# Score tiles in three shared PSUM banks and a second bank for filling work, in the grouped-query attentions of a two-layer trunk

## The chip, the cores and the metric

One core of one Trainium2 chip runs the whole program in one launch. The metric is the device time of one execution in microseconds (us); lower is better. TensorE does the matrix products, VectorE (DVE), ScalarE (ACT) and GpSimd (POOL) the elementwise work, SyncE (SP) issues most of the DMAs.

## The reference, cut to what matters

Two layers of a parallel-branch trunk over 512 latent tokens and 256 context tokens, width 1024. Each layer normalises and modulates the tokens, projects them once, runs a neighbourhood attention (A) and a grouped-query attention (B, 8 heads of 64 channels, keys of 256 context and 512 latent tokens), multiplies each branch by its own SiLU gate path, projects and merges. The second layer updates the latent tokens alone. What the change touches is branch B:

```
def _attend(q, k, v):
    s = jnp.einsum('bqkgd,btkd->bkgqt', q, k).astype(jnp.float32) * (HEAD_DIM ** -0.5)
    p = jax.nn.softmax(s, axis=-1).astype(v.dtype)
    return jnp.einsum('bkgqt,btkd->bqkgd', p, v)
...
qb = _rope_2d(_rmsnorm(hs(b_q, GQA_Q_HEADS), q_norm_b), pos_row, pos_col)
b_att = _gqa_latent(qb, k_all, v_all)     # latent queries: 768 keys
...
o_a = (a_att * jax.nn.silu(a_z)) @ w_o_a
o_b = (b_att * jax.nn.silu(b_z)) @ w_o_b
merged = jax.nn.sigmoid(g_a) * o_a + jax.nn.sigmoid(g_b) * o_b
return merged @ w_out
```

In the first layer the 256 context queries also attend, to the 256 context keys.

## The kernel before

All products of float32 data are made of two or three products of high and low parts (`mm3`: L435, L436, L437), so TensorE has most of the work.

The grouped-query attention of a layer goes head by head, heads 0 to 7. For a head, `gq_scores` makes four **score tiles** of 128 queries by 768 keys, here called i0 to i3. A tile is four matmuls (L886 and L887, high and low keys; 512 and then 256 columns, since one matmul writes at most one PSUM bank of 512 float32). VectorE then reads the tile for its row maximum (L1157), ScalarE reads it again for the exponential (L1158, with the row sum read out behind it), ScalarE casts the result to fp16 (`h`, L837), and VectorE (i0 and i2) or GpSimd (i1 and i3, `SPLIT_POOL`) makes the fp16 **low part** (L838). SyncE turns the pair by a transposing DMA (`ht<-h`, L842). When all four tiles of the head are turned, `gq_values` spreads the reciprocal row sums by four small transposes (`divide`, L849) and makes the head's **values** by twelve matmuls (L1174 and L1175), which ScalarE and VectorE then gather (`head_out`, L824 and L825). The first layer has a fifth, smaller score tile for each head: `ctx_scores`, 256 context queries by 256 keys in a 512-column tile, with its maximum (L899, L901), two exponentials (L905) and `ctx_values` (L921).

Between the heads stands **filling work** (`fill`): the rest of the gate projections (`g_chunks`, out of `hx` tiles) and branch A's output projection (`o_chunks("a", ...)`, out of `gah` and `gal`), in pieces (`chan_proj`) of 24 or 12 matmuls that each accumulate in one PSUM bank and are then emptied by ScalarE's tanh (L625) or VectorE's multiply (L703). `pipeline` writes the order of the program: scores of head h, values of head h-1, an eighth of the filling pieces; before the last head's values it writes what is left of them.

The written order isn't the order that runs. A scheduler in the build simulates the program and sets the order on each engine by it; what is ready earliest goes first. It also sets the semaphores: an instruction waits for the last reader of a PSUM region that it overwrites, and regions of one tile that lie in the same bank are not told apart.

PSUM has eight banks for each partition. Throughout, `f` (1 bank, filling) and `t` (2 banks, transposes and values) stay open; `open_ps` opens the other five for each stage. In the grouped-query attentions these are two score tiles of 1024 columns, of which 768 are used (`s`, 4 banks), and `v` (1 bank). `psw` hands out the banks of projections in turn from `f` and the `x` banks; there are no `x` banks here, so all filling pieces take `f`, but for one that `v_for` sends to `v`.

Of the kernel before, what the change touches and what calls it, by code (L numbers as in the profile page):

```python
# [72 lines left out]
def hybrid_kernel(es: ExitStack, tc, x, ctx, cvec, w_ada, w_ada0, small, gvec, w_in, w_o_a, w_o_b, w_out,  # L73
# [13 lines left out]
    def nm(s):  # L87
        uid[0] += 1
        return f"{s}_{uid[0]}"
# [4 lines left out]
    pm = {}  # L94

    def ps_pool(stack, kind, bufs, cols):
        pool = tc.tile_pool(name=nm("ps" + kind), bufs=bufs, space=bass.MemoryType.PSUM, reuse_waits="tile")
        pm[kind] = (stack.enter_context(pool), cols)
# [6 lines left out]
    def open_ps(x=0, **kinds):  # L105

        if "es" in pm:
            pm["es"].close()
        pm["es"] = ExitStack()
        pm["n"], pm["i"], pm["v_for"] = x + 1, 0, ()  # L110
        if x:
            kinds["x"] = (x, 512)
        for kind, (bufs, cols) in kinds.items():
            ps_pool(pm["es"], kind, bufs, cols)

    def psw(n=512, kind="w"):
        if kind == "w":
            kind = "f" if pm["i"] % pm["n"] == 0 else "x"
            pm["i"] += 1
            if pm["i"] in pm["v_for"]:  # L120
                kind = "v"
        pool, cols = pm[kind]
        return pool.tile([128, cols], F32, tag=kind, name=nm("ps" + kind))[:, :n]
# [154 lines left out]
    def ada_steps(l, tiles, halves, nv, pool, queue=None):  # L278

        cb = {}  # L280

        def load(h):
            cb[h] = pool.tile([128, 2, 512], F32, tag="cb", name=nm("cb"), bufs=1)
            for v in range(nv):
                src = cd[8 * v + 4 * h:8 * v + 4 * h + 4].rearrange("k p -> (k p)").unsqueeze(0)
                nc.sync.dma_start(cb[h][:, v, :], src.to_broadcast([128, 512]))

        def load_tile(h, i):
            cb["w"] = pool.tile([128, 512], F32, tag="rawb", name=nm("rawb"), bufs=2)
            (queue or nc.sync).dma_start(cb["w"], w_ada[l, h, i])  # L290

        def dot(h, i, v):
            if v == 0:
                load_tile(h, i)
            w = cb["w"]
            o = w if v == nv - 1 else pool.tile([128, 512], BF16, tag="junk", name=nm("junk"), bufs=1)
            behind(ON_DVE, lambda: V.tensor_tensor_reduce(o, w, cb[h][:, v, :], 1.0, 0.0, ALU.mult, ALU.add,
                                                          asum[:, i, h, v:v + 1]))
        res = []
        for h in halves:  # L300
            res += [lambda h=h: load(h)] + [lambda h=h, i=i, v=v: dot(h, i, v) for i in tiles for v in range(nv)]
        return res
# [6 lines left out]
    def ada_mod(l):  # L309
        mod_finish(l, ada_sum(0, 16, 2).rearrange("p (a k) v -> p a k v", a=2), 0, 8)  # L310
# [179 lines left out]
    def run(fill, n):  # L490
        for _ in range(min(n, len(fill))):
            fill.pop(0)()
# [102 lines left out]
    def layer(l, hx, nxt, start):  # L595
        first = l == 0
# [7 lines left out]
        def gate_steps(halves, pool):  # L604
            return (ada_steps(l, range(16, 24), halves, nv, pool)
                    + ([lambda: ada_gate(l, nv, pool)] if 1 in halves else []))
# [9 lines left out]
        att = {}  # L616
# [90 lines left out]
        if first:  # L707
            w, pss = start()
# [21 lines left out]
            bg = ada_steps(1, range(16), (0,), 2, hp["p"])  # L730
        else:
# [5 lines left out]
            bg = gate_steps((0, 1), hp["p"])  # L737
# [49 lines left out]
        if True:  # L787
            def softmax_tail(p, n, r, total, pieces, on_act=False):

                V.reciprocal(r, r)  # L790
                V.tensor_scalar(r, r, P_UP, None, ALU.mult)
                for i, (c0, c1) in enumerate(pieces):
                    if on_act:
                        S.activation(p[:, c0:c1], p[:, c0:c1], AF.Copy, scale=r[:, i:i + 1])
                    else:
                        V.tensor_scalar(p[:, c0:c1], p[:, c0:c1], r[:, i:i + 1], 0.0, ALU.mult, ALU.add,
                                        accum_out=total[:, 1:2])
# [85 lines left out]
            def scores(ps, q, kh, kl, cuts):  # L883

                for c0, n, sl in cuts:
                    T.matmul(ps[:, c0:c0 + n], q, sl(kh), start=True, stop=False)  # L886
                    T.matmul(ps[:, c0:c0 + n], q, sl(kl), start=False, stop=True)  # L887

            def cut(a, b):
                return lambda k: k[:, a:b]  # L890

            def ctx_scores(q, kh, kl, ct, late=True):

                pss = ps_score()
                for i in range(2):
                    scores(pss, q[:, 512 + 128 * i:640 + 128 * i], kh, kl,
                           [(256 * i, 256, cut(512, 768))])
                mx = sp.tile([128, 2], F32, tag="mx", name=nm("mx"), bufs=8)
                V.tensor_reduce(mx, pss.rearrange("p (i n) -> p i n", i=2), AX, ALU.max, negate=True)  # L899
                if late:  # L900
                    V.tensor_scalar(mx, mx, P_LOG, None, ALU.add)  # L901
                p = p_tile()
                r = sp.tile([128, 2], F32, tag="r", name=nm("r"), bufs=8)
                for i in range(2):
                    S.activation(p[:, 256 * i:256 * i + 256], pss[:, 256 * i:256 * i + 256], AF.Exp,  # L905
                                 bias=mx[:, i:i + 1], accum_out=r[:, i:i + 1])
                if not late:
                    softmax_tail(p, 512, r, mx, [(0, 256), (256, 512)])
                turned(p, 512, ct.rearrange("p a i k n -> p (a i k) n"), G)
                return ct, r  # L910
# [14 lines left out]
            def p_tile():  # L925
                return att["p"].tile([128, att["w"]], F32, tag="p", name=nm("p"), bufs=att["np"])

            def ps_score(n=512):
                return psw(n, "s")
# [83 lines left out]
            def pipeline(fill, spread, scores_of, values_of, last=None, bg=[]):  # L1013

                n = len(fill)
                prev = None
                for h in range(8):
                    att["bg"] = bg if h > 3 or pm["n"] == 1 else []
                    st = scores_of(h)
                    if prev is not None:  # L1020
                        values_of(h - 1, prev)
                    run(fill, len(fill) - (n - n * min(h + 1, spread) // spread))
                    prev = st
                if last is not None:
                    run(fill, len(fill))
                    last()
                run(bg, len(bg))
                att["spare"] = True
                values_of(7, prev)
                run(fill, len(fill))  # L1030
# [24 lines left out]
            bg = []  # L1055
# [43 lines left out]
            bg = gate_steps((0,), hp["p"]) if first else []  # L1099
# [38 lines left out]
                turn_late(1 if i == 0 else 0)  # L1138
            bp_es.close()
            gq_es = open_att(f"gq{l}", 768, NP_GQ[l], 0, NH_GQ[l])  # L1140
            open_ps(s=(2, 1024), v=(1, 512))
            if first:
                pm["v_for"] = (2,)
            nc.sync.dma_start(zb.rearrange("p (f n) -> p f n", f=4)[:, :, :ntok], zs[:, :, :ntok])
            V.memset(vbig[:, 2950:2951], -P_LOG)
            lift = vbig[:, 2950:2951].to_broadcast([128, 768])
# [1 line left out]
            def gq_scores(q, kh, kl):  # L1148
                ht = att["p"].tile([128, 4, 12, 128], F16, tag="ht", name=nm("ht"), bufs=2)
                r = att["p"].tile([128, 4], F32, tag="r4", name=nm("r4"), bufs=3)  # L1150
                for i in range(4):
                    pss = ps_score(768)
                    scores(pss, q[:, 128 * i:128 * i + 128], kh, kl,
                           [(0, 512, cut(0, 512)), (512, 256, cut(512, 768))])
                    p = p_tile()
                    mx = sp.tile([128, 2], F32, tag="mx", name=nm("mx"), bufs=8)
                    V.tensor_tensor_reduce(p, pss, lift, -1.0, 3e38, ALU.add, ALU.min, mx[:, 0:1])  # L1157
                    S.activation(p, pss, AF.Exp, bias=mx[:, 0:1], accum_out=r[:, i:i + 1])  # L1158
                    turned(p, 768, ht[:, i], G if i in SPLIT_POOL else V)
                    run(att["bg"], 1)  # L1160
                return ht, r
# [38 lines left out]
            bg = gate_steps((1,), Parts(att["p"], own)) if first else []  # L1200
# [3 lines left out]
        with tc.tile_pool(name=f"mrg{l}", bufs=1, reuse_waits="tile") as mp:  # L1204
# [34 lines left out]
            bg = ada_steps(1, range(16), (1,), 2, mp, G) + [lambda: ada_mod(1)] if first else []  # L1239
            run(bg, 1)  # L1240
            per_bg = -(-len(bg) // nt)
            for n in range(2):
# [14 lines left out]
                late = []  # L1257
# [187 lines left out]
    def nxt():  # L1445
        if not hx1:
            hx1.extend([[big("hx") for _ in range(2)] for _ in range(2)])
        return hx1
    layer(0, hx0, nxt, start)
    layer(1, hx1, None, None)  # L1450


# [73 lines left out]
```

## Time and profile before

| | us |
|---|---|
| median of 3 runs (lowest, highest) | 1110.4 (1109.44, 1111.03) |
| the profiled execution | 1110.55 |
| its span in the trace | 1108.8 |
| TensorE busy | 1074.5 (97%) |
| VectorE, ScalarE, GpSimd busy | 767.4, 617.2, 470.1 |
| first grouped-query attention, in the trace | about 374 to 545 |
| second grouped-query attention | about 920 to 1040 |

The page gives busy time by engine. A view by windows gives it for a stretch, with the clock that the throttle granted to TensorE (1.00 is full). The view of waits adds up how long an engine stood idle before a group of instructions and what ended that. In rows of the timeline the first number is the start and the second the duration, in us; matmuls overlap their neighbours, so the distance between two starts, not the duration, is what one costs.

### The profile page before, as it was taken

Reading aid. Unit: us, or ns where it says so; the run is one execution under the profiler, and the core shown is the slowest. Engines: PE = TensorE matmul, PEld = TensorE weight load, DVE = VectorE, ACT = ScalarE, POOL = GpSimd, SP = SyncE. Lnnn points to the kernel's source line nnn. Section 1 sums busy time; section 2 is a strip of 40 time slices with the busy share of each in tenths; the row PEclk is TensorE's granted clock in tenths of the full one; section 3 lists DMA queues with packets and bytes.
Section 4 is the critical chain, followed back from the end, with each engine's and each line's share of the span. In section 5 each row is a group of like instructions: output and inputs, shape, how many; then the busy total and the mean of one; then the engine's idle time right before and its main releaser. Section 6 shows DMA issues by size and latency. Waiting matters only on the chain. (4 is left out here: it accounts for less than half of the span.)

```text
span 1108.8 us, 16943 instructions
## 1 busy us (share of the span) xinstructions
PE 1074.5 (97%) x5672; PEld 876.9 (79%) x5672; DVE 767.4 (69%) x1600; ACT 617.2 (56%) x1236; POOL 470.1 (42%) x397
## 2 busy tenths in 40 slices
PE   8999999899999999979999999999999999999998
PEld 6688888788888877757788878888877888777677
DVE  5567799974378478676577785466997665777473
ACT  6464279776333566655330275444899446786430
POOL 1044235554256244454521455232355472564531
PEclk9999999999999999989999999999999999999999
DMA  9454325554543498769533542453565536879642
GB/s 374 153 169 143 91 70 116 125 137 121 174 141 117 132 205 185 172 185 271 171 105 125 166 136 82 138 165 99 132 148 130 156 106 171 200 232 236 188 152 77
DMA packets 236001, 171.79 MB, mean 155 GB/s; under 512 B 160141, under 2 KB 201865, under 8 KB 234249
## 3 DMA queue, kind: packets, MB, share of 16 engines
q1 hardware_dynamic: 228576, 156.31, 51.7%
q0 software_dynamic: 2368, 7.87, 2.2%
q10 hardware_dynamic: 4968, 6.53, 1.8%
q8 instruction: 45, 0.74, 0.3%
q14 instruction: 44, 0.35, 0.1%
HBM read 115.58 MB, written 17.32 MB: 120 GB/s over the span
## 5 line engine op out<-in xcount | busy, mean ns | idle before, releaser
L838 POOL TENSOR_TENSOR h<-p,h 128x256 f16<-128x256 f32 (+2 forms) x104 | 113.1, 1096 | 167.7 <-ACT h L837 119.9
L422 POOL TENSOR_TENSOR wlo<-raw,whi 128x512 fp32r<-128x512 f32 x70 | 98.8, 1416 | 124.5 <-ACT whi L420 80.9
L435 PE MATMUL psf<-hx,whi 128*128 128x512 f32 (+1 forms) x360 | 137.5, 382 | 2.5 <-ACT zt L625 1.3
L437 PE MATMUL psf<-hx,wlo 128*128 128x512 f32 (+1 forms) x360 | 135.5, 376 | 0.0
L436 PE MATMUL psf<-hx,whi 128*128 128x512 f32 (+1 forms) x360 | 135.4, 376 | 0.0
L435 PE MATMUL psx<-whi,hx 128*128 128x512 f32 (+1 forms) x328 | 121.0, 372 | 0.0
L420 ACT CAST whi<-raw 128x512 fp32r<-128x512 f32 x136 | 82.9, 620 | 67.5 <-DMA raw<-in_w_in_dram 48.3
L437 PE MATMUL psx<-whi,hx 128*128 128x512 f32 (+1 forms) x328 | 120.0, 367 | 0.0
L436 PE MATMUL psx<-wlo,hx 128*128 128x512 f32 (+1 forms) x328 | 119.6, 366 | 0.0
L408 POOL TENSOR_TENSOR wlo<-raw,whi 128x512 fp32r<-128x512 f32 x40 | 59.5, 1489 | 119.2 <-ACT whi L405 76.0
L405 ACT CAST whi<-raw 128x512 fp32r<-128x512 f32 x88 | 54.2, 623 | 96.8 <-PE psx L437 34.2
L508 POOL TENSOR_TENSOR ss<-ss,ehalf 128x8 f32<-128x8 f32 (+2 forms) x40 | 63.6, 1593 | 77.8 <-DVE ss L505 72.5
L422 DVE TENSOR_TENSOR wlo<-raw,whi 128x512 fp32r<-128x512 f32 x66 | 70.8, 1073 | 35.2 <-ACT whi L420 34.1
L837 ACT CAST h<-p 128x256 f16<-128x256 f32 (+2 forms) x136 | 81.6, 616 | 7.7 <-DMA ct<-h 3.7
L435 PEld LDWEIGHTS psf<-hx,whi 128*128 128x128 f32 x360 | 67.8, 188 | 15.1 <-ACT zt L625 2.5
L1157 DVE CUSTOM_DVE_ANT_0 p<-pss,vb 128x768 f32<-128x768 f32 x64 | 60.4, 954 | 25.4 <-PE pss L887 22.7
L1158 ACT ACTIVATE p<-pss,mx 128x768 f32<-128x768 f32 x64 | 57.6, 901 | 35.7 <-DVE mx L1157 34.8
L437 PEld LDWEIGHTS psf<-hx,wlo 128*128 128x128 f32 x360 | 67.8, 188 | 11.8
L436 PEld LDWEIGHTS psf<-hx,whi 128*128 128x128 f32 x360 | 67.9, 189 | 10.7
L437 PEld LDWEIGHTS psx<-whi,hx 128*128 128x128 f32 x328 | 61.9, 189 | 10.2
L436 PEld LDWEIGHTS psx<-wlo,hx 128*128 128x128 f32 x328 | 62.0, 189 | 9.4
L435 PEld LDWEIGHTS psx<-whi,hx 128*128 128x128 f32 x328 | 61.8, 189 | 9.1 <-issue 0.2
(338 smaller groups left out, 2972.4 us busy)
## 6 DMA issues: line engine op xcount, KB each, us to landing
raw<-in_w_in_dram SPq DMA_DIRECT2D x168, 256.0 KB, 2.9
rawb<-in_w_ada_dram SPq DMA_DIRECT2D x48, 256.0 KB, 2.8
raw<-in_w_out_dram SPq DMA_DIRECT2D x32, 256.0 KB, 2.9
tg<-gs SPq DMA_DIRECT2D x4, 1536.0 KB, 7.1
rawx<-in_w_ada_dram SPq DMA_DIRECT2D x4, 1024.0 KB, 10.7
rawy<-in_w_ada_dram SPq DMA_DIRECT2D x4, 1024.0 KB, 9.3
gs<-zt ACTq DMA_DIRECT2D x16, 256.0 KB, 2.9
raw<-in_w_o_a_dram SPq DMA_DIRECT2D x16, 256.0 KB, 3.1
```

Source lines behind the costliest of these rows:

```text
L405: S.copy(hi[:, :n], raw[:, :n])
L408: e.tensor_tensor(lo[:, :n], raw[:, :n], F(hi[:, :n]), ALU.subtract)
L420: S.copy(hi, raw)
L422: lo_eng(i).tensor_tensor(lo, raw, F(hi), ALU.subtract)
L435: T.matmul(ps, lhs[0], rhs[0], start=first, stop=False)
L436: T.matmul(ps, lhs[0], rhs[1], start=False, stop=False)
L437: T.matmul(ps, lhs[1], rhs[0], start=False, stop=last)
L508: G.tensor_tensor(ss, ss, ehalf[:, :n], ALU.pow)
L837: S.copy(h[:, 0], p[:, :n])
L838: eng.tensor_tensor(h[:, 1], p[:, :n], h[:, 0], ALU.subtract)
L1157: V.tensor_tensor_reduce(p, pss, lift, -1.0, 3e38, ALU.add, ALU.min, mx[:, 0:1])
L1158: S.activation(p, pss, AF.Exp, bias=mx[:, 0:1], accum_out=r[:, i:i + 1])
```

## The change

The two score slots become the halves of one tile of 1536 columns, three banks: slot 0 is columns 0 to 767, slot 1 columns 768 to 1535. The middle bank (512 to 1023) holds the last 256 columns of slot 0 and the first 256 of slot 1; each slot's two pieces are cut at the bank's edge, so slot 1 is written 256 columns first. Slots are taken in turn (`ps_slot`), the context tile too. The bank that this frees becomes an `x` bank, so that filling pieces alternate between two banks; `v_for` goes. The condition on `bg` only keeps its meaning where the number of `x` banks no longer tells it. Nothing is tied to keep VectorE's low parts behind other work. From here on the lines of the file move down by up to six: the maximum becomes L1163, the exponential L1164, the values L1180 and L1181.

```
@@ ctx_scores
-                pss = ps_score()
+                pss = ps_slot()[0][:, 0:512] if late else ps_score()
...
@@ pipeline
-                    att["bg"] = bg if h > 3 or pm["n"] == 1 else []
+                    att["bg"] = bg if h > 3 or last is not None else []
...
@@ the grouped-query attention
-            open_ps(s=(2, 1024), v=(1, 512))
-            if first:
-                pm["v_for"] = (2,)
+            open_ps(x=1, s=(1, 1536), v=(1, 512))
+            slots = psw(1536, "s")
+            turn_of = [0]
+
+            def ps_slot():
+
+                i = turn_of[0] % 2
+                turn_of[0] += 1
+                return slots[:, 768 * i:768 * i + 768], (512, 256)[i]
...
@@ gq_scores
-                    pss = ps_score(768)
+                    pss, m = ps_slot()
                     scores(pss, q[:, 128 * i:128 * i + 128], kh, kl,
-                           [(0, 512, cut(0, 512)), (512, 256, cut(512, 768))])
+                           [(0, m, cut(0, m)), (m, 768 - m, cut(m, 768))])
```

No instruction is added or removed on any engine; the scheduler puts them in another order. Two places show it, both in the second layer.

TensorE before, at head 5's first two tiles. `pss` are score tiles, `pst<-ident,r` the spread reciprocals, `psf<-gah` filling work; the brackets name the engines whose semaphores the instruction waits for:

```order
L886 MATMUL pss_10581<-gk_9240,qs_10576 128x512 [waits PE_49,Activation_49]
L887 MATMUL pss_10581<-gk_9240,qs_10576 128x512
L886 MATMUL pss_10581<-gk_9240,qs_10576 128x256
L887 MATMUL pss_10581<-gk_9240,qs_10576 128x256
L886 MATMUL pss_10594<-gk_9240,qs_10576 128x512 [waits PE_49,Activation_49]
L887 MATMUL pss_10594<-gk_9240,qs_10576 128x512
L886 MATMUL pss_10594<-gk_9240,qs_10576 128x256
L887 MATMUL pss_10594<-gk_9240,qs_10576 128x256
L849 MATMUL pst_10633<-ident,r_2149_10459 128x128 [waits DVE_49]
L849 MATMUL pst_10633<-ident,r_2149_10459 128x128 x3
L435 MATMUL psf_10657<-gah_10548,whi_10389 128x512 [waits DVE_49]
L436 MATMUL psf_10657<-gal_10549,whi_10389 128x512
```

TensorE after, from head 4's last tile to head 5's first two; all are parts of the one tile `pss_9813`:

```order
L886 MATMUL pss_9813<-gk_9205,qs_10408 128x256 [waits Activation_49]
L887 MATMUL pss_9813<-gk_9205,qs_10408 128x256
L886 MATMUL pss_9813<-gk_9205,qs_10408 128x512
L887 MATMUL pss_9813<-gk_9205,qs_10408 128x512
L886 MATMUL pss_9813<-gk_9205,qs_10525 128x512 [waits Activation_49]
L887 MATMUL pss_9813<-gk_9205,qs_10525 128x512
L886 MATMUL pss_9813<-gk_9205,qs_10525 128x256
L887 MATMUL pss_9813<-gk_9205,qs_10525 128x256
L849 MATMUL pst_10578<-ident,r_2097_10412 128x128 [waits DVE_49,PE_49]
L849 MATMUL pst_10578<-ident,r_2097_10412 128x128 x3
L886 MATMUL pss_9813<-gk_9205,qs_10525 128x256 [waits Activation_49]
L887 MATMUL pss_9813<-gk_9205,qs_10525 128x256
```

Before, tiles stood in pairs with a filling piece behind each pair, and the value of ScalarE's semaphore was that of the exponential two tiles back. Now no filling work stands between the tiles here, and the value that each tile waits for is that of the exponential of the tile just ahead of it, in either slot.

VectorE before, around a maximum (`ISA p,mx<-pss`, L1157, with the read-out behind it) and the low parts (`h<-p,h`) there, in the second layer:

```order
L1157 ISA p_2192_10612,mx_2193_10613<-pss_2191_10607,vb_1882_9238 128x768
L1157 ISA mx_2193_10613 128x1
L838 TENSOR_TENSOR h_2186_10590<-p_2184_10586,h_2186_10590 128x768
L1157 ISA p_2196_10625,mx_2197_10626<-pss_2195_10620,vb_1882_9238 128x768
L1157 ISA mx_2197_10626 128x1
```

VectorE after, at a head's tiles i2 and i3:

```order
L1163 ISA p_2159_10675,mx_2160_10676<-pss_1967_9813,vb_1844_9203 128x768
L1163 ISA mx_2160_10676 128x1
L838 TENSOR_TENSOR h_2161_10679<-p_2159_10675,h_2161_10679 128x768
L1163 ISA p_2162_10687,mx_2163_10688<-pss_1967_9813,vb_1844_9203 128x768
L1163 ISA mx_2163_10688 128x1
L847 RECIPROCAL r4_2152_10646<-r4_2152_10646 128x4
```

Before, the low part between two maxima belonged to an older tile (`p_2184`); now it belongs to the tile whose maximum stands right ahead of it (`p_2159`).

## The prediction

> **What bounds the kernel now.** I began with the page: which engine is busy, and whether its clock is full.
>
> ```profile
> PE 1074.5 (97%) x5672; PEld 876.9 (79%) x5672; DVE 767.4 (69%) x1600; ACT 617.2 (56%) x1236; POOL 470.1 (42%) x397
> PEclk9999999999999999989999999999999999999999
> ```
>
> TensorE is busy 97% of the span, so the time is TensorE's work plus its idle time, plus what a slower clock costs. The change adds and removes no matmul. It can only move the idle time and the clock, so next I read the stretches that it touches by windows (busy time of each engine, then the clock), and four short ones around the dip in the clock.
>
> ```profile
> 374.00:545.00 171.00, 156.54 (x867) 124.71 (x866) 119.52 (x209) 106.04 (x205) 80.36 (x56) 0.97 0.76 185
> 920.00:1040.00 120.00, 116.60 (x550) 88.74 (x550) 81.43 (x130) 83.70 (x150) 64.70 (x43) 1.00 0.86 213
> 481.28:484.70 3.42, 1.38 (x8) 0.78 (x7) 3.32 (x6) 3.35 (x7) 3.42 (x3) 1.00 0.86 338
> 484.70:488.11 3.41, 2.92 (x7) 2.15 (x7) 3.41 (x1) 3.36 (x9) 3.41 (x3) 0.50 1.08 418
> 491.52:494.94 3.42, 1.38 (x5) 1.19 (x6) 2.52 (x6) 0.00 (x0) 1.35 (x2) 0.50 0.28 62
> 494.94:498.35 3.41, 3.41 (x11) 2.70 (x9) 2.27 (x3) 0.99 (x2) 0.49 (x1) 0.50 0.31 71
> ```
>
> Idle: 171.00 - 156.54 = 14.5 us in the first attention, 120.00 - 116.60 = 3.4 in the second. The clock was half in three windows that held 2.92 + 1.38 + 3.41 = 7.7 us of busy time, so half of that, 3.9 us, was lost. Together 22 us: no change to these two stretches can gain more. The waits of TensorE, first attention and then second, say what the idle time was for.
>
> ```profile
> PE psv L849 <- DVE ho L825: 5.8, 1, 5.8
> PE psf L435 <- ACT zt L625: 2.0, 2, 1.6
> PE pss L886 <- ACT p L905: 1.3, 1, 1.3
> PE psf L435 <- DVE tg L703: 1.2, 3, 0.5
> PE pss L886 <- ACT p L1158: 0.9, 1, 0.9
> ...
> PE psf L435 <- ACT zt L625: 0.9, 2, 0.5
> PE psf L435 <- DVE tg L703: 0.7, 2, 0.5
> PE pss L886 <- ACT p L1158: 0.5, 1, 0.5
> ```
>
> A filling piece waited for its only bank 2.0 + 1.2 + 0.9 + 0.7 = 4.8 us; a score tile waited for an exponential only 1.3 + 0.9 + 0.5 = 2.7 us. Both resources that the change trades are nearly free now.
>
> **The second filling bank.** It takes away the 4.8 us. It also changes when filling work runs: with one bank a piece had to wait until the last was emptied, with two the scheduler finds one ready almost always and puts it into every space. In the changed order the first attention has filling work up to head 4's tile i1, and from there to the last values only nine stray matmuls of branch B's projection; in the second it ends at head 3's i0, and nine stray ones follow up to head 7's last tile. Until then at least 4 us of other matmuls stand between most tiles. Behind that point the tiles stand alone.
>
> **The shared bank.** Each tile now waits for the exponential of the tile just ahead. What one such step costs, from rows: the spacing of a tile's matmuls; then a tile whose maximum and exponential met no queue; then a score matmul released by an exponential, with the cast behind it.
>
> ```profile
> 379.05 0.40 PE L886 MATMUL pss<-gk,qs 128*128 128x512 f32 x1
> 379.75 0.40 PE L435 MATMUL psf<-hx,whi 128*128 128x512 f32 x1
> ...
> 374.66 0.28 PE L887 MATMUL pss<-gk,qs 128*128 128x256 f32 x1
> 374.98 0.96 DVE L1157 CUSTOM_DVE_ANT_0 p<-pss,vb 128x768 f32<-128x768 f32 x1 [1.34 <-PE pss L887]
> 375.98 0.90 ACT L1158 ACTIVATE p<-pss,mx 128x768 f32<-128x768 f32 x1 [3.06 <-DVE mx L1157]
> ...
> 436.32 0.90 ACT L1158 ACTIVATE p<-pss,mx 128x768 f32<-128x768 f32 x1
> 437.34 0.83 ACT L837 CAST h<-p 128x768 f16<-128x768 f32 x1
> 437.36 0.39 PE L886 MATMUL pss<-gk,qs 128*128 128x256 f32 x1 [0.91 <-ACT p L1158]
> ```
>
> A tile takes 379.75 - 379.05 = 0.70 us of issue. From its end, 374.94, to the exponential's end, 376.88, are 1.94 us, and 437.36 - 437.22 = 0.14 more to the next tile's first matmul: 2.1 us in which TensorE stands still if nothing else is queued ahead of that tile. What TensorE does in between is taken off.
>
> In the changed order a low part of VectorE stands between the maxima of i0 and i1, and of i2 and i3. It needs the cast, which begins 0.12 us after the exponential (437.34 - 437.22).
>
> ```profile
> L838 DVE TENSOR_TENSOR h<-p,h 128x768 f16<-128x768 f32 x14 | 14.7, 1053 | 10.3 <-ACT h L837 10.3
> L838 POOL TENSOR_TENSOR h<-p,h 128x768 f16<-128x768 f32 x15 | 26.2, 1746 | 33.7 <-ACT h L837 21.2 <-issue 6.7 <-PE psf L437 5.1
> L899 DVE TENSOR_REDUCE mx<-pss 128x2 f32<-128x512 f32 x7 | 4.8, 689 | 3.6 <-PE pss L887 3.5
> L901 DVE TENSOR_SCALAR mx<-mx 128x2 f32<-128x2 f32 x7 | 3.0, 428 | 0.1
> L905 ACT ACTIVATE p<-pss,mx 128x256 f32<-128x256 f32 x14 | 6.5, 470 | 9.6 <-DVE mx L901 9.6
> ht<-h SPq DMA_TRANSPOSE x30, 3.7
> 392.25 0.39 PE L1174 MATMUL pst<-ht,vb 128*128 128x512 f16 x1 [0.74 <-DMA ht<-h]
> 394.64 0.38 PE L1175 MATMUL pst<-ht,vb 128*128 128x512 f16 x1
> ```
>
> The low part ends 0.12 + 0.83 + 0.04 + 1.05 = 2.04 us behind the exponential; without it the next maximum could start at 0.14 + 0.86 + 0.04 = 1.04 (0.86 is the tile from its first start to its last end). So it adds 1.0, and a step across it costs 3.1. A step behind the context tile: 0.69 + 0.43 + 2 x 0.47 and some 0.2 of gaps, 2.3.
>
> The values follow as a wait of their own: they need tile i3 turned. From the end of i3's matmuls: 1.0 (the low part of i2) + 1.94 + 0.12 + 0.83 + 1.75 on GpSimd + 3.7 for the DMA from issue to landing (the median of 30) = 9.4 us with 0.1 for gaps. Ahead of the values stand the next head's i0 and i1, 3.1 + 0.86 + 2.1 + 0.86 = 6.9 us. So they wait 2.5. Twelve matmuls at (394.64 - 392.25) / 11 = 0.217 are 2.6 us.
>
> **The sum, second attention.** A head without filling work: i1 to i2, 3.1 less the values' 2.6, 0.5; i2 to i3, 2.1; i3 to the next i0, 3.1; i0 to i1, 2.1 less 0.4 for the spread, 1.7; values, 2.5. That is 9.9 us of standing for 5.8 of work. Heads 3 and 4 pay it whole (19.8). Head 5 has five filling matmuls in the way (1.1, so 8.8), head 6 three (0.7, so 9.2). Head 7: 0.5 + 2.1 + 3.1 for its values behind 6.3 us of branch B's products, 5.7. The start in head 2 and 3: 1.4 + 2.2. Total 47.
>
> **First attention.** The context tile is a fifth step. Head 4 from its i1: 1.0 + 2.7 + 1.9 + 2.4 = 8.0. Head 5: 2.1 + 2.1 + 3.1 + 1.9 + 2.4 = 11.6. Head 6, where 0.4 to 0.9 of other work stands in some steps: 9.8. Head 7: 1.7 + 2.1 + 3.1, and 5.0 for its values with no tiles ahead: 11.9. After that branch B's products wait some 2 for the last head's channels. Total 43.
>
> **The front parts**, where filling work is dense: steps there need 2.1 to 3.1 and mostly have 4 to 7 us of cover; a few have 1.1 to 2.8. I put 5 + 2 us, between zero and the 18 us of today. Were that cover gone too, a head would cost the 9.9 of the tail.
>
> **The clock.** The longest gap in the first of the four short windows is in this row of the timeline.
>
> ```profile
> 483.76 0.49 PE L435 MATMUL psf<-gah,whi 128*128 128x512 f32 x1 [1.60 <-ACT zt L625]
> ```
>
> So half clock followed a window that was busy 1.38 of 3.42 us (40%), with no single gap over 1.6 in it; one with 2.92 of 3.41 (86%) brought it back. A tail head is busy about 5.8 of 15.7 us, 37%, so the clock should fall, and come back in part where values and tiles run together. Whole heads at half clock would cost 2.6 for the values and 0.7 for each of i2 and i3, 4.0 us (i0 and i1 only eat up the values' wait); at full clock nothing. I take half, 2.0, for nine heads: 18 us, from 0 to 36.
>
> The Trainium skill, on the page "TensorE: Matmul & The Clock Gate", section "Why this matters for your kernels", asks for no TensorE gap over about 3 us. By that rule alone the tails, with gaps of 2 to 3, would keep the clock and the sum would be 18 us lower. The row above, 40% busy with short gaps, speaks against it.
>
> **Forecast.** The profiled execution's own time is 1110.55 us (span 1108.8; the median is 1110.4). 1110.55 + 47 + 43 + 7 - 22 + 18 = **1203.5 us**.
>
> **The rivals.**
> 1. The clock stays full in the tails: 1203.5 - 18 = 1185.5. For it: at 37 to 50% the rows between 40% and 86% are missing. Chance 0.22.
> 2. The clock is half throughout the tails and the turning DMAs stay at the slow end: 1203.5 + 18 = 1221.5, and some more. For it: the 0.50 lasted a whole window after TensorE was fully busy again (494.94 to 498.35). Chance 0.2.
>
> ```profile
> L1158 ACT ACTIVATION_READ_ACCUMULATOR p<-pss,mx 128x1 f32 x32 | 6.2, 193 | 0.0
> L879 ACT CAST qs<-qb 64x512 fp32r<-64x512 f32 x8 | 4.9, 616 | 4.1 <-PE pss L887 4.0
> L824 ACT COPY ho<-pst 64x512 f32<-64x512 f32 x6 | 3.5, 582 | 1.4 <-PE pst L1175 1.3
> ```
>
> 3. The slots are two, as the words say: the wait is by columns, not by bank, and a tile is written while the other is read. The steps go, and a tail head is bound by ScalarE, 4 x (0.90 + 0.19 + 0.83) + 0.62 + 0.58 = 8.9 against 5.8 us, 3.1 more for five heads. In the first layer the context tile adds some 2.5 there and 1.2 on TensorE, so 4.4 more, for not quite four heads. That is 32 in place of 90, and no 18: 1127.5. Against it: the built program's semaphore values are those of the exponential just ahead, in both slots. The Trainium skill's page "PSUM — Partial Sum Buffer", section "PSUM bank collisions raise a hardware error", says that the wait has to be by bank and quadrant and not by address; by that rule the forecast's sum stands. Chance 0.03.
> 4. Faster: cover lasts. Where over 2.1 us of other matmuls stand ahead of each tile, a step costs nothing, and the 4.8 + 2.7 us of today's waits on banks go: 1103. It decides at the place where filling work ends; the changed order shows 29 of 70 distances between tiles under 2.2 us, nearly all behind it, so this needs tails that are not there. Chance 0.02.
>
> The forecast's own case has 0.52, and 0.01 is left for no change. A measurement of this kernel tells about 0.2% (2 us) from no change. So faster 0.02, same 0.01, slower 0.97.
>
> **The range.** Down: full clock (-18), the fastest turning DMAs (0.5 for each of nine values, -5), no stalls in the front beyond 2 (-5), and 10 for steps that overlap better than added up: 1165. Up: half clock throughout (+18), slow DMAs (+8), and the first attention's 5.8 us wait behind VectorE back again (+6), 5 for queues on VectorE: 1240. It holds rivals 1 and 2.
>
> **What would show it.** Right: TensorE's waits `pss L886 <- ACT p L1164` grow from 1.4 us to some 50; VectorE's maxima wait for TensorE's scores; values wait for `DMA ht<-h` two to three us in each tail head; `psf L435 <- ACT zt` is gone; TensorE's busy share falls to about 90%; the PEclk digits dip in the slices that hold the two tails, and the front heads run without idle time. Wrong: few waits on L1164, or full clock with 37% busy windows (then 1185), or filling work that still runs beside heads 5 to 7.

## The result and the profile after

| | before | after |
|---|---|---|
| median, us (lowest, highest) | 1110.24 (1109.44, 1111.03) | 1213.18 (1210.77, 1213.9) |
| profiled execution, us | 1110.55 | 1213.9 |
| its span | 1108.8 | 1211.7 |
| TensorE busy | 1074.5 | 1113.7 |
| TensorE idle (span less busy) | 34.3 | 98.0 |

The changed kernel takes 1.0923 times as long (95% interval 1.0904 to 1.0942), 102.9 us more. 1203.5 us was forecast, 1165 to 1240 as the range. Shown first are two groups of the page before, a score tile's maximum and exponential. Then come lines of the page after: its busy time, the clock digits, and the groups on either side of a score tile. Behind the second bar stands the idle time of the engine ahead of the group, and what ended it:

```profile
L1157 DVE CUSTOM_DVE_ANT_0 p<-pss,vb 128x768 f32<-128x768 f32 x64 | 60.4, 954 | 25.4 <-PE pss L887 22.7
L1158 ACT ACTIVATE p<-pss,mx 128x768 f32<-128x768 f32 x64 | 57.6, 901 | 35.7 <-DVE mx L1157 34.8
```

```profile
PE 1113.7 (92%) x5672; PEld 893.1 (74%) x5672; DVE 761.3 (63%) x1600; ACT 622.9 (51%) x1236; POOL 463.9 (38%) x397
...
PEclk9999999999999998967699999999999999867799
...
L886 PE MATMUL pss<-gk,qs 128*128 128x256 f32 (+1 forms) x144 | 60.1, 426 | 54.2 <-ACT p L1164 47.7
L1164 ACT ACTIVATE p<-pss,mx 128x768 f32<-128x768 f32 x64 | 57.7, 901 | 100.0 <-DVE mx L1163 99.8
...
L1163 DVE CUSTOM_DVE_ANT_0 p<-pss,vb 128x768 f32<-128x768 f32 x64 | 61.1, 954 | 50.4 <-PE pss L887 45.5
```

Read the last three rows as a ring: a tile's matmuls waited 47.7 us for the exponential (L1164), the exponential 99.8 us for the maximum (34.8 before), the maximum 45.5 us for the tile's matmuls (22.7 before). Three engines wait for one another. TensorE's count of matmuls is the same, so its 39.2 us more of busy time is the same work at a slower clock.

Where that time lies, by windows (busy time of TensorE first, the clock third from the right): the first attention before and behind the end of filling work, the second one likewise.

```profile
374.00:456.00 82.00, 79.98 (x468) 68.13 (x466) 38.17 (x70) 42.19 (x81) 25.27 (x19) 1.00 0.57 151
456.00:605.00 149.00, 109.74 (x496) 79.10 (x497) 88.34 (x155) 70.34 (x135) 60.62 (x44) 0.79 0.61 162
...
950.00:1040.00 90.00, 89.48 (x412) 71.13 (x411) 41.54 (x61) 46.22 (x80) 41.98 (x29) 1.00 0.69 183
1040.00:1150.00 110.00, 71.35 (x242) 43.05 (x241) 48.49 (x84) 49.85 (x85) 32.88 (x23) 0.74 0.49 115
```

Each attention begins dense and at full clock (80.0 of 82 us, 89.5 of 90) and ends with TensorE busy 65 to 75% at three quarters of the clock. From the first score matmul to the last values, the first attention grew from 165.8 us (374.1 to 539.9) to 216.0 (375.5 to 591.5), the second from 120.5 (923.5 to 1044.0) to 178.1 (969.4 to 1147.5).

The waits of TensorE, first attention and then second, and its waiting matmuls in the second tail, with one exponential, as the timeline has them (start, duration, and in brackets the idle time before and what ended it):

```profile
PE pss L886 <- ACT p L1164: 19.3, 10, 2.6
PE pss L886 <- ACT p L905: 6.4, 3, 2.7
PE psf L436 <- POOL gal L668: 4.9, 3, 2.8
PE pst L320 <- DVE ag L318: 2.1, 1, 2.1
...
PE pss L886 <- ACT p L1164: 28.4, 14, 2.8
PE pst L1180 <- DMA ht<-h: 5.8, 5, 2.5
```

```profile
1080.65 0.39 PE L886 MATMUL pss<-gk,qs 128*128 128x256 f32 x1 [2.78 <-ACT p L1164]
...
1083.83 0.80 PE L886 MATMUL pss<-gk,qs 128*128 128x512 f32 x1 [2.22 <-ACT p L1164]
...
1097.62 0.39 PE L886 MATMUL pss<-gk,qs 128*128 128x256 f32 x1 [2.65 <-ACT p L1164]
...
1100.34 0.90 ACT L1164 ACTIVATE p<-pss,mx 128x768 f32<-128x768 f32 x1 [1.10 <-DVE mx L1163]
...
1101.38 0.80 PE L886 MATMUL pss<-gk,qs 128*128 128x512 f32 x1 [2.79 <-ACT p L1164]
```

A bare step took 1083.83 - 1080.65 = 3.18 us from tile to tile, one across a VectorE low part 1101.38 - 1097.62 = 3.76. The prediction had 0.86 + 2.1 = 2.96 and 0.86 + 3.1 = 3.96.

The last two rows show more than the change was written for. The matmul at 1101.38 is the first piece of a tile in slot 0, 512 columns, and it started 0.14 us behind the end of slot 1's exponential (1100.34 + 0.90 = 1101.24). Yet it writes columns 0 to 511, the first of the three banks, and slot 1 lies in the other two. So the waits in the built order are wider than a rule by bank: regions of the one tile aren't told apart even where they share no bank.

The clock in the same place:

```profile
1059.20:1062.60 3.40, 0.87 (x5) 0.57 (x3) 1.56 (x3) 1.51 (x3) 1.26 (x1) 1.00 0.00 0
1062.60:1076.30 13.70, 9.45 (x25) 5.10 (x26) 6.43 (x11) 6.98 (x12) 2.84 (x2) 0.50 0.38 86
1076.30:1083.10 6.80, 2.53 (x12) 1.48 (x10) 2.98 (x6) 3.64 (x7) 1.71 (x2) 1.00 0.26 58
1083.10:1093.40 10.30, 7.79 (x21) 4.15 (x22) 4.93 (x9) 5.16 (x9) 2.75 (x2) 0.50 0.69 109
```

It falls behind stretches that were 26 to 37% busy (0.87 of 3.40, 2.53 of 6.80) and comes back behind some that were 69 to 76% busy at half clock, over and over, with no wait over 2.8 us among those above. (Elsewhere in this tail, it fell behind a stretch that was 51% busy, 5.25 of 10.20 us from 1107.00 on, and came back behind one of 66%, 6.75 of 10.30 from 1117.20 on.) That is what the prediction took from the kernel before, and the rule that it weighed against it (no gap over about 3 us) did not hold here. The same page of the Trainium skill, "TensorE: Matmul & The Clock Gate", section "A second HAM failure mode: psum-queue depth-cycling", tells of a kernel in which frequent short idle times made the clock go back and forth; these rows agree with that one.

### The profile page after: what moved, and what is told of

Same layout as the page of the kernel before. It is cut to its first block, busy times and chain, and to the rows that moved or that the text cites. A ratio compares the mean times of both kernels' runs of the same rounds, so it can differ in the third digit from the quotient of the medians.

```text
span 1211.7 us, 16933 instructions
## 1 busy us (share of the span) xinstructions
PE 1113.7 (92%) x5672; PEld 893.1 (74%) x5672; DVE 761.3 (63%) x1600; ACT 622.9 (51%) x1236; POOL 463.9 (38%) x397
## 5 line engine op out<-in xcount | busy, mean ns | idle before, releaser
L838 POOL TENSOR_TENSOR h<-p,h 128x256 f16<-128x256 f32 (+2 forms) x104 | 108.8, 1054 | 213.8 <-ACT h L837 127.0
L422 POOL TENSOR_TENSOR wlo<-raw,whi 128x512 fp32r<-128x512 f32 x70 | 99.3, 1422 | 131.4 <-ACT whi L420 101.8
L886 PE MATMUL pss<-gk,qs 128*128 128x256 f32 (+1 forms) x144 | 60.1, 426 | 54.2 <-ACT p L1164 47.7
L1164 ACT ACTIVATE p<-pss,mx 128x768 f32<-128x768 f32 x64 | 57.7, 901 | 100.0 <-DVE mx L1163 99.8
L435 PE MATMUL psf<-hx,whi 128*128 128x512 f32 x272 | 107.7, 396 | 1.2 <-DVE zt L627 1.2
L437 PE MATMUL psf<-hx,wlo 128*128 128x512 f32 x272 | 107.2, 394 | 0.0
L436 PE MATMUL psf<-hx,whi 128*128 128x512 f32 x272 | 107.2, 394 | 0.0
L405 ACT CAST whi<-raw 128x512 fp32r<-128x512 f32 x88 | 54.2, 622 | 99.0 <-PE psx L437 37.6
L435 PE MATMUL psx<-hx,whi 128*128 128x256 f32 (+1 forms) x304 | 98.7, 325 | 0.0
L437 PE MATMUL psx<-hx,wlo 128*128 128x256 f32 (+1 forms) x304 | 98.6, 324 | 0.0
L436 PE MATMUL psx<-hx,whi 128*128 128x256 f32 (+1 forms) x304 | 98.5, 324 | 0.0
L422 DVE TENSOR_TENSOR wlo<-raw,whi 128x512 fp32r<-128x512 f32 x66 | 60.6, 918 | 53.6 <-ACT whi L420 53.5
L1163 DVE CUSTOM_DVE_ANT_0 p<-pss,vb 128x768 f32<-128x768 f32 x64 | 61.1, 954 | 50.4 <-PE pss L887 45.5
L886 PEld LDWEIGHTS pss<-gk,qs 128*128 128x128 f32 x144 | 32.2, 223 | 69.0 <-ACT p L1164 57.4
L437 PEld LDWEIGHTS psx<-whi,hx 128*128 128x128 f32 x328 | 61.9, 189 | 10.4
## 6 DMA issues: line engine op xcount, KB each, us to landing
rawx<-in_w_ada_dram SPq DMA_DIRECT2D x4, 1024.0 KB, 10.3
```

The lines of the kernel that those rows point to most:

```text
L422: lo_eng(i).tensor_tensor(lo, raw, F(hi), ALU.subtract)
L435: T.matmul(ps, lhs[0], rhs[0], start=first, stop=False)
L436: T.matmul(ps, lhs[0], rhs[1], start=False, stop=False)
L437: T.matmul(ps, lhs[1], rhs[0], start=False, stop=last)
L838: eng.tensor_tensor(h[:, 1], p[:, :n], h[:, 0], ALU.subtract)
```

## Experiments

Theory 1 was the prediction's: the shared bank makes the tiles serial, and each step costs 2 to 3 us where no other matmul stands ahead of it. Its rivals were the second filling bank, the missing ties of VectorE's low parts, and a serial chain that sets the time wherever the filling work lies. Line numbers shift from kernel to kernel: in those below the exponential of a score tile is L1156 to L1193, the context tile's is L905 or L915.

### Half of the change: the shared bank, and the second filling bank

```
-            open_ps(x=1, s=(1, 1536), v=(1, 512))
+            open_ps(s=(1, 1536), v=(1, 512))
+            if first:
+                pm["v_for"] = (2,)
```

> The shared three-bank tile alone, without the second filling bank (the bank that comes free is left unused). Theory 1 (tiles made serial by the shared bank pay wherever no other matmul stands ahead of them; the second bank only brings the end of the filling work forward): the built order has filling work up to tile 26 of 40 in the first attention and tile 18 of 32 in the second, against 23 and 13 in the changed kernel, so 25 bare steps in place of 33; of the 103 us lost, 25/33 or some 78 stay: 1165 to 1195 us, with `psf L435 <- ACT zt` back at 3 to 8 us. Theory 2 (the second bank spends the filling work early, and that is the cause): the filling work keeps its old pace, 1108 to 1120 us.

Measured: 1211.21 us, ratio 1.0902 (1.0887 to 1.0917). That can't be told from the whole change (1.0904 to 1.0942). TensorE's waits, first attention and then second:

```profile
PE pss L886 <- ACT p L1166: 17.8, 9, 3.7
PE psf L435 <- DVE tg L703: 5.2, 6, 2.2
...
PE psf L435 <- ACT zt L625: 3.3, 5, 0.8
...
PE pss L886 <- ACT p L1166: 19.7, 10, 2.8
PE pst L1182 <- DMA ht<-h: 7.0, 4, 4.6
PE psf L435 <- DVE tg L703: 3.8, 3, 2.3
...
PE psf L435 <- ACT zt L625: 2.4, 2, 1.5
```

The three-bank tile alone, without the second filling bank, makes the whole loss. Theory 1's 1165 to 1195 us was still a miss: it counted the bare steps that the later end of the filling work saves, and not what one filling bank costs. The waits for exponentials in these rows are 47.7 - 37.5 = 10 us shorter than after, and those for the only filling bank (`psf` behind `tg` and `zt`) come to 14.7.

The other half puts the slots back into banks of their own and keeps the second filling bank; the context values go to the transposes' banks:

```
-            open_ps(s=(2, 1024), v=(1, 512))
-            if first:
-                pm["v_for"] = (2,)
+            open_ps(x=1, s=(2, 1024))
...
-                ps = psw(512 if late else 256, "v" if late or not att["spare"] or pm["n"] > 1 else "s")
+                ps = psw(512 if late else 256, "t" if late else "v")
```

> The second filling bank alone: score slots stay in banks of their own (two of two banks each), bank v goes, and the context values use the transposes' banks. Theory 1 (serial tiles are the cause): a tile waits for the exponential two tiles back, TensorE keeps filling work to the end of both attentions, the filling pieces' waits of 4.8 us go: 1103 to 1114 us. Theory 2 (greedy use of the second bank is the cause): bare steps at the ends of both attentions, clock at half there, 1140 us or more.

Measured: 1113.44 us, ratio 1.0020 (1.0005 to 1.0034); TensorE is 97% busy by the page, and the view of waits has one wait for a score tile's exponential in the two attentions:

```profile
PE 1072.7 (97%) x5672; PEld 877.4 (79%) x5672; DVE 764.8 (69%) x1600; ACT 617.4 (56%) x1236; POOL 468.7 (42%) x397
```

```profile
PE pss L886 <- ACT p L1156: 2.0, 1, 2.0
```

So the second filling bank is not what spent the cover. The two halves together settle what made the loss: the slots as halves of one tile that share a bank. The Trainium skill's page "PSUM — Partial Sum Buffer" (the section named in the prediction) says that engines have to be kept apart by bank; slot 1 waiting for slot 0's exponential, with only 256 of its columns in the middle bank, agrees. Slot 0 waiting for slot 1's exponential with a piece in a bank of its own (1101.38 above) goes beyond that. No run had the slots as parts of one tile but in banks of their own, so whether the common bank or the common tile makes the tiles serial stays open.

### The low parts of VectorE

```
                     V.tensor_tensor_reduce(p, pss, lift, -1.0, 3e38, ALU.add, ALU.min, mx[:, 0:1])
+                    ties = latest(ON_DVE, 1)
...
-                    turned(p, 768, ht[:, i], G if i in SPLIT_POOL else V)
+                    held.append(lambda p=p, i=i: turned(p, 768, ht[:, i], G if i in SPLIT_POOL else V))
+                    if i in SPLIT_POOL:
+                        behind(ON_DVE, held.pop(0), ties)
+                        held.pop(0)()
```

> The changed kernel with VectorE's low part of i0 and of i2 tied behind the next tile's maximum. Theory 1 (the shared bank makes the loss, the low part in front of the maximum lengthens two steps of a head by 1.0 us): about 9 tail heads x 2 x 1.0, some of it taken by the values that wait for the turned tiles, longer where the clock is half: 8 to 20 us less than the changed kernel, 1193 to 1205 us. Rival (what is missing is the tie of VectorE's low parts, and most of the loss comes from there): 1110 to 1150 us.

Measured: 1207.13 us, ratio 1.0867 (1.0853 to 1.0881), 6 us less than the changed kernel: the rival is out, and theory 1's 8 to 20 was too much. Two groups of VectorE, maximum and low part, the changed kernel's and then this one's (busy time, mean ns, idle time before and what ended it):

```profile
L1163 DVE CUSTOM_DVE_ANT_0 p<-pss,vb 128x768 f32<-128x768 f32 x64 | 61.1, 954 | 50.4 <-PE pss L887 45.5 <-PE psx L436 2.5 <-POOL wlo L422 1.2
...
L838 DVE TENSOR_TENSOR h<-p,h 128x768 f16<-128x768 f32 x32 | 35.5, 1109 | 38.1 <-ACT h L837 37.9
```

```profile
L1164 DVE CUSTOM_DVE_ANT_0 p<-pss,vb 128x768 f32<-128x768 f32 x64 | 61.1, 955 | 96.0 <-PE pss L887 91.0 <-issue 2.4 <-POOL gal L668 1.3
...
L838 DVE TENSOR_TENSOR h<-p,h 128x768 f16<-128x768 f32 x32 | 32.8, 1025 | 0.0
```

VectorE no longer waits 37.9 us for the cast, but 91.0 in place of 45.5 for the matmuls. In the bare steps the tile behind has to wait for the ring anyway.

### Cover put back, in three steps

Now the changed kernel's filling work was moved and nothing else. First whole pieces (2.7 or 5.4 us), tied on TensorE behind the score tiles:

```
+                    left = att["all"] - att["all"] * att["tile"] // 32
+                    while len(att["fill"]) > left:
+                        behind(ON_PE, att["fill"].pop(0))
```

> The changed kernel with the filling pieces tied on TensorE between the score tiles, evenly by count, so that they last to the end of both attentions. The pieces are of 2.7 or 5.4 us, so the spread is lumpy: 22 of 70 distances between tiles still hold under 1 us of other matmuls. Theory 1 (a bare step costs 2 to 3 us, a covered one nothing): 1110 - 22 + 22 x 2.5 = 1143, say 1120 to 1155 us, with the clock full in nearly all of both attentions, since no stretch of several tiles is bare. Rival (the chain tile, maximum, exponential, tile sets the time whatever lies between): 1195 to 1215 us.

Measured: 1202.57 us, ratio 1.0830 (1.0813 to 1.0847). By its number this was the rival's. But the test was a poor one: 20 waits for a score tile's exponential remained (8 and 12; 24 after), of 47.3 us in all. The waits of the first attention and then the second:

```profile
PE pss L886 <- ACT p L1166: 19.7, 8, 3.6
PE pst L1186 <- DMA ht<-h: 9.3, 4, 3.2
...
PE pss L886 <- ACT p L1166: 27.6, 12, 4.9
```

A piece of 5.4 us ahead of one tile gives nothing to the bare step behind it. So the pieces were cut into steps of three matmuls, and `few` writes as many steps as are due by a tile, each tied behind what stands last on TensorE (`STEPS` counts the steps of an attention, 192 and 96):

```
+        def step(k):
+            mm3(ps, (wh(k, 0), wh(k, 1)), (act(k, 0), act(k, 1)), k == 0, k == nk - 1)
+            if k == nk - 1:
+                evac(f, n0, n1, ps)
...
+                    few(STEPS[l] * att["tile"] // 32) 
```

> The changed kernel with the filling work cut into steps of three matmuls (some 0.7 us) and these tied on TensorE between the score tiles, evenly: in the built order 61 of 70 distances between tiles hold at least 1.9 us of other matmuls. Theory 1 (a bare step costs 2 to 3 us, a covered one nothing; the earlier spread by pieces of 2.7 and 5.4 us failed because 22 distances stayed bare): 1110 - 22 + 9 bare steps x 2.2 + what the 3.1 us steps lack behind 2.0 us of cover, 16 x 1.0 = 1124, say 1110 to 1140 us, clock full throughout. Rival (the serial chain sets the time wherever the filling work lies): 1195 to 1215 us.

Measured: 1169.76 us, ratio 1.0527 (1.0500 to 1.0555). The same steps with the low parts tied:

> The same as the run before it, with VectorE's low parts of i0 and i2 tied behind the next tile's maximum as well. Theory 1: the 16 x 1.0 us that those steps lack go: 1100 to 1125 us, 5 to 16 us less than without the tie; this would be the shared bank at its best. If low parts in front of maxima don't matter once cover is there: within 3 us of the run without the tie. Rival (serial chain): about 1200 us.

Measured: 1149.43 us, ratio 1.0335 (1.0315 to 1.0356). And with a share of the steps behind the context tile:

```
                 turned(p, 512, ct.rearrange("p a i k n -> p (a i k) n"), G)
+                if late:
+                    att["tile"] += 1
+                    few(STEPS[l] * att["tile"] // 40)
```

> The shared bank with tied steps and low parts tied, and now a share of the steps behind the first layer's context tile too, where 0.4 us of other matmuls stood and TensorE waited 18.1 us in seven waits for the context tile's exponential. The steps are taken from distances that held 3 to 6 us. Theory 1 (each step pays what its own cover lacks): those waits fall under 4 us and no others grow by more than 4: 1130 to 1141 us. Rival (the chain of a head sets its time, so the wait only moves to the next tile): 1145 to 1152 us, with the same sum of waits under other names.

Measured: 1141.8 us, ratio 1.0282 (1.0259 to 1.0305), just above theory 1's range and below the rival's. The waits for exponentials in the first attention, without the share behind the context tile and with it; the last row is the second attention's, with it:

```profile
PE pss L896 <- ACT p L915: 18.1, 7, 3.5
...
PE pss L896 <- ACT p L1190: 0.2, 1, 0.2
```

```profile
PE pss L896 <- ACT p L1193: 8.1, 12, 1.3
PE pss L896 <- ACT p L915: 4.9, 4, 2.1
...
PE pss L896 <- ACT p L1193: 13.8, 19, 2.0
```

The 18.1 us became 4.9, not under 4, and 8.1 came back in twelve small waits at the tiles that gave steps away, more than the 4 that theory 1 allowed. The same filling work, only moved, gave back 1213 - 1170 = 43 us, with the tie 64 and with the context tile 71: there is no chain that costs about 1200 wherever the filling work lies. But the runs with steps alone and with the tie came out 30 and 24 us above theory 1's ranges, and the tie was worth 20 us, more than the 5 to 16 expected. So theory 1's sums were too low: that a step with cover costs nothing is not borne out as it stands. The second attention still has 19 waits of 0.7 us: its spaces hold about 2.0 us and a step asks for up to 3.1, while the values, which fall into one space of four, are more than that one needs. That there is hardly enough cover for serial tiles is argued from these spaces and not shown by a run.

### The price of the half clock

```
+                    if not first and att["tile"] > 13:
+                        def dummy():
+                            pd = psw(512, "v")
+                            for _ in range(8):
+                                T.matmul(pd, q[:, 128 * i:128 * i + 128], kh[:, 0:512], start=True, stop=True)
+                        behind(ON_PE, dummy, tied)
```

> The changed kernel with eight products behind each score tile of the second attention from tile 14 on, into the idle bank v, which nothing reads (about 1.9 us of TensorE in a gap of 2.1 to 3.1; they do no part of the computation). The filling work stays where it was, and the first attention is unchanged. Of the second attention's tail the half clock took 21 us (42.0 us of busy time at half clock). If the half clock is on the path: the clock returns to 1.00 there and the time falls by 8 to 20 us, less what the products stand in the way of values, to 1195 to 1206 us. If the half clock only fills waits that are there anyhow: 1209 to 1218 us.

Measured: 1207.23 us, ratio 1.0868 (1.0845 to 1.0891). The same window of the second tail, after and then here:

```profile
1049.00:1141.10 92.10, 56.50 (x172) 32.61 (x173) 38.63 (x67) 42.43 (x71) 28.93 (x20) 0.69 0.46 101
```

```profile
1049.00:1141.10 92.10, 81.52 (x367) 57.28 (x366) 37.56 (x67) 41.24 (x69) 27.91 (x19) 0.99 0.47 107
```

The clock went from 0.69 to 0.99, and the time fell by 6 us, where counting lost busy time said 21. Both expectations missed: neither 8 to 20 nor nothing. So at least 6 of the 21 us were on the path. That the rest lay in time that TensorE would have waited anyway is likely but not shown, since the added products cost something too: an exponential ended at 1098.57 (1097.67 + 0.90), and the next tile started only at 1099.92, with no wait, behind eight products and five filling matmuls.

### A kernel that beats both

These four are made of edits shown above, on the kernel with the second filling bank alone: the steps of three matmuls (`step`, `few`), the tie of the low parts, or both; the last goes back to one filling bank.

> For a kernel that beats both: score slots in banks of their own, the second filling bank (as in the run with the filling bank alone), the filling work in tied steps of three matmuls, and VectorE's low parts tied behind the next maximum. Theory 1: a tile waits for the exponential two tiles back, and every pair of distances holds over 4 us, so only the waits for the last values are left of the 22 us that can be gained: 1096 to 1108 us. Against it: tied steps leave the scheduler less to choose from, and a step that waits for a weight part or for its bank's emptying holds up the tiles behind it: 1110 to 1120 us.

Measured: 1101.4 us, ratio 0.9908 (0.9892 to 0.9924). Which part does it, by leaving out the steps, the tie, and the second bank:

> Score slots in banks of their own and the second filling bank, with VectorE's low parts tied behind the next maximum, filling work free. If the tie gives the 10 us by which the best kernel so far is faster than the kernel before (low parts in front of maxima): 1098 to 1105 us. If the tied steps give them: 1109 to 1116 us, as without the tie.

> Score slots in banks of their own, the second filling bank and the filling work in tied steps, low parts free. If the tied steps give the 10 us (an even cover, so no wait for an exponential two tiles back and no half clock): 1098 to 1105 us. If the tie of the low parts does: 1109 to 1116 us.

> The kernel before with the filling work in tied steps and the low parts tied, but one filling bank. If the second bank is needed for the gain (a piece waits until the one bank is emptied, 4.8 us before, and now holds up the tied steps behind it): 1106 to 1116 us. If the order alone makes it: 1098 to 1105 us.

Measured: ties without steps 1124.49 us (1.0112, 1.0099 to 1.0126), slower, which neither side expected. Steps without ties **1099.18 us (0.9884, 0.9870 to 0.9897)**, the best of all. Steps and ties with one filling bank 1106.45 us (0.9953, 0.9940 to 0.9965). So the gain comes with the steps. With steps, the tie makes no clear difference (1101.4 and 1099.18, their intervals overlap), and the second bank is worth 1106.45 - 1101.4 = 5.0 us, once the slots don't share one. The best kernel's TensorE, and all its waits for score exponentials, first attention and then second:

```profile
PE 1070.2 (98%) x5672; PEld 875.3 (80%) x5672; DVE 756.5 (69%) x1600; ACT 617.5 (56%) x1236; POOL 462.3 (42%) x397
```

```profile
PE pss L896 <- ACT p L1180: 1.6, 2, 1.3
...
PE pss L896 <- ACT p L1180: 0.2, 1, 0.2
```

Its idle time is 1096.8 - 1070.2 = 26.6 us, 7.7 less than before, and TensorE is busy 4.3 us less for the same matmuls.

## Why the prediction was right, step by step

- **Serial tiles, each step 2.1 to 3.1 us of idle time.** Right, and shown: tile to tile 3.18 and 3.76 us against 2.96 and 3.96 (the step from i2 to i3, priced at 2.1, stood 2.65 and 2.78 in the rows above, since VectorE's `ho`, 0.68 us at 1094.99, comes ahead of i2's maximum); 47.7 us of waits on L1164 against "some 50"; TensorE 92% busy against about 90%; the front parts without idle time; the clock down in the two tails alone.
- **The second filling bank takes away 4.8 us.** The wait for `ACT zt` is gone, and with slots of their own the bank was worth 5.0 us.
- **The second filling bank spends the filling work early.** This reason was wrong. The built order ends its filling work early with one filling bank too (at tile 26 of 40 and 18 of 32), and that kernel takes 1211.2 us; the second bank alone loses next to nothing (1113.4 us). That the holes between serial tiles draw the filling work in is the reading that fits both. The sum didn't suffer, since it was made from the order, not from the reason.
- **Values wait 2.5 us a head.** Too much: 5.8 us in five waits, 1.2 each. The head as a whole came out right: the exponentials of i0 of heads 4 to 7 start at 1069.2, 1086.5, 1104.1 and 1122.2, periods of 17.3 to 18.1 us against 15.7 + 2.0. In part that is luck. From head 5's i0 (1083.83) to head 6's (1101.38), 17.55 us, TensorE stood 1.23 + 0.55 + 2.65 + 2.79 = 7.2 us where the sum has 9.9, and its matmuls took 10.3 where it has 5.8 + 2.0. The half clock stretched more of them, and that filled part of the waits.
- **The sum by attention.** Second: 47 + 2 - 3.4 and 10 for the clock is 55.6, measured 178.1 - 120.5 = 57.6. First: 43 + 5 - 18.4 + 8 = 37.6, measured 50.2. But some of these 50.2 us are work that moved: before, 48 matmuls of branch A's projection ran behind the first attention's last values (from 540.25 on), and after, all of them run ahead. At their spacing there, 24 of 0.23 us and 24 of 0.12, they are some 8.4 us (an estimate), which leaves 41.8 and a miss of 4. Most of it comes off again outside: from the last values of the first attention to the first score of the second 383.6 us before, 377.9 after. The first attention also has waits that the prediction did not have, in the rows above: 4.9 us for GpSimd's `gal`, because the filling work reached branch A's output projection before its input was ready, and 2.1 for `ag`.
- **Standing and clock apart.** TensorE's idle time grew from 165.80 - 151.72 = 14.1 us to 216.00 - 176.70 = 39.3 in the first attention and from 120.50 - 117.10 = 3.4 to 178.10 - 138.92 = 39.2 in the second, by 61.0 together. The sum, without its terms for the clock, has 97 - 17.9 = 79. The rest of the loss shows as busy time. So the number was nearer than its parts, which is luck in part: more work ran at the slow clock than the sum had, and less time was spent standing. Longer matmuls fill waits, so the trace alone doesn't price the two apart.
- **Clock, 18 us for nine heads.** That the clock falls was right; rival 1 (full clock) is out, and so is rival 2 (half throughout), by 0.79 and 0.74 over the tails. In the second attention 10 was forecast, and 6 came back with the clock kept up, less what the added products cost; for the first attention it wasn't measured.
- **Rivals 3 and 4.** Two free slots: out, by the waits, and the kernel with slots of their own shows what that would have given. Lasting cover in the shared bank: the three runs above tried it, and the best reached 1141.8, not 1103. The claim there, that a step with over 2.1 us of cover costs nothing, leaves out the low part and the context tile: the tie alone was worth 20 us there.
- **The limit of 22 us.** The best kernel gains 12.7, inside it.

## What to carry to other kernels

Two slots cut from one PSUM tile so that they share a bank were one buffer to this build's scheduler: count the ring of writer, reader, reader before giving a bank away, and ask whether other work of that length stands in every step. Work that hides waits should be dealt out in small tied steps as even as the waits are; beside serial tiles, left to a scheduler that takes whatever is ready, it was gone before the end, and in big pieces it left steps bare. Price a slow clock by a run that keeps it up, not by the busy time that it stretches.

## What the runs showed of the hardware

A VectorE instruction that elsewhere takes about 1 us or less can take 5 to 8 us. One each, of the kernel before (a low part of a weight, 1.07 us on average there) and of the one with the second filling bank alone (128x2 elements, 0.43 us on average in the prediction's row of the kernel before), each followed by the GpSimd row beside it:

```profile
483.66 8.22 DVE L422 TENSOR_TENSOR wlo<-raw,whi 128x512 fp32r<-128x512 f32 x1
482.98 7.12 POOL L668 TENSOR_TENSOR gal<-za,gah 128x768 fp32r<-128x768 f32 x4
```

```profile
529.86 5.60 DVE L901 TENSOR_SCALAR mx<-mx 128x2 f32<-128x2 f32 x1
530.11 5.32 POOL L668 TENSOR_TENSOR gbl<-zb,gbh 128x768 fp32r<-128x768 f32 x3
```

In both GpSimd ran several instructions back to back in that time, and the VectorE instruction ended 1.8 us behind their end in the one (491.88 and 490.10; GpSimd's next instruction, L422, ran on to 491.32) and with it in the other (535.46 and 535.43). The Trainium skill, page "GPSIMD Engine Reference", section "1. Specifications", says that the two share memory interfaces when VectorE reads two tensors or works in a two-port mode; the first row, with two tensors read, agrees; the second reads one, and its mode isn't in the trace. No run took the neighbour away to prove it. DMA traffic alone doesn't explain it: in the kernel with ties and without steps such an instruction (503.06, 5.81 us) ran on while the DMA engines moved nothing (0 GB/s from 504 to 508). In the kernel before, this stands ahead of TensorE's wait of 5.8 us for `ho` and of two of its three windows at half clock (1.38 + 3.41 us busy, so 2.4 us lost). The best kernel's attentions have no such instruction, nor have the changed kernel's (the longest take 2.60 and 2.57 us); the kernel with ties and without steps has two (5.81 and 7.94 us). How much of the best kernel's 12.7 us and of that one's loss comes from this and how much from even cover stays open.
